# Weight halves in one tile, their columns in groups of four at a distance of sixteen, in ten of twenty units

## The chip, the cores and the metric

The kernel runs on one core of a Trainium2 chip. The metric is the device time of one execution in microseconds (us), the median of several runs.

## The reference

The reference is one attention layer with a normalisation on either side. There are 256 tokens of width 4096 and 32 heads of 128 columns, all in float32.

```python
xn   = rms_norm(x, norm_attn)                 # (256, 4096)
q, k, v, g = split(xn @ w_in_attn, 4)         # w_in_attn: 4096 x 16384
o    = stick_breaking_attention(q, k, v)      # 32 heads, strictly causal, suffix sums in log space
h    = x + (o * silu(g)) @ w_out_attn         # w_out_attn: 4096 x 4096
out  = rms_norm(h, final_norm)
```

The convolution weights of the inputs are not used at this depth. Nearly all the arithmetic lies in the two products with `w_in_attn` and `w_out_attn`.

## The kernel before

**Units and steps.** The columns of the weights are worked off in twenty units: units 0 to 15 are `w_in` (one unit holds q, k, v and gate columns of two heads), units 16 to 19 are `w_out`. A unit covers two by two blocks, and the 4096 rows are worked off in sixteen steps of 256. Units 0 and 16 ("plain") use the ordinary eight block products a step; the other eighteen ("mixed") use a scheme of seven products in most steps (Strassen's kind) and eight products in the rest. In a mixed unit of `w_in`, ten steps have seven products and six steps have eight, 118 in all. Each product is a 128x128 form of the activations (the stationary operand) times 512 weight columns (the moving operand), added up in one of seven PSUM banks `acc`.

**High and low parts.** A float32 factor is split in two parts of type fp32r, the high one and the rest, and `mm3` makes one product out of three matmuls: high by high, high by low, low by high. The weights come as `raw` tiles by DMA. In `piece` ScalarE copies `raw` to `wh` (a cast to fp32r) and VectorE subtracts, `wl = raw - wh`. A tile pair `wh`, `wl` has one or two blocks (`size` 1 or 2) of W = 512 columns, which are two halves (i = 0, 1) of CW = 256 columns from different places of the weight matrix. `split` allots them: five buffers of size 2 (tag "w"), two of size 1 (tag "s"). In steps of seven products `sums` forms three sums on VectorE in the `raw` tiles, and GpSimd issues an accumulating DMA for a fourth.

**Order.** All instructions go through a planner (`Plan`), which simulates the engines with fixed costs (`vector_ns`, `scalar_ns`, `tensor_ns`) and writes the program in the order that the simulation gives. An engine then runs its list in that order, with the waits that the data ask for. The planner's price of a matmul of n columns is

```python
def tensor_ns(n):
    return 0.4167 * n + 13.4 if n > 128 else 109.0
```

**Around it.** While unit u is multiplied, the two heads of unit u-1 are worked off between its matmuls (transposes `tr`, scores and scan `z`, output `o`), and VectorE and ScalarE empty the PSUM banks (`combine`) and do the softmax-like part. Every engine call is recorded by one helper, so all instructions bear line L121 in the profile; groups are told apart by their tiles.

Of the kernel before, what the change touches and what calls it, by code (L numbers as in the profile page):

```python
# [11 lines left out]
F32R = mybir.dt.float32r  # L12
# [7 lines left out]
P = 128  # L20
# [5 lines left out]
CW = 256  # L26
HG = CW // P
NB = D // CW
W = 2 * CW
# [27 lines left out]
ON_SCALAR = ((1, 3, 5), (1, 3))  # L57
AHEAD, SUMS_AHEAD = 4.0, 3.0
BLOCKS_LATER = 2


PLAIN = {"C11": 1, "C21": 6, "C12": 7, "C22": 3}
# [22 lines left out]
def plain_part(k, one, two):  # L85

    return k, BOTH, ((one, "A11", 0), (two, "A21", 0), (one, "A12", 1), (two, "A22", 1))
# [150 lines left out]
def kernel(  # L238
# [14 lines left out]
    wp = ctx.enter_context(tc.tile_pool(name="weights", bufs=1))  # L253
# [5 lines left out]
    ap = rooms.enter_context(tc.tile_pool(name="attention", bufs=1))  # L259
# [4 lines left out]
    def minus(out_, full, part):  # L264
        nc.vector.tensor_tensor(out=out_, in0=full, in1=part.bitcast(F32), op=ALU.subtract)
# [14 lines left out]
    for u, (kind, w, cols) in enumerate(units):  # L280
        for s in (step_at(u, k) for k in range(NS)):
            quads.append(tuple((w, c, s) for c in cols))
            if kind == "plain":
                which = [plain_part(0, PLAIN["C11"], PLAIN["C21"]), plain_part(1, PLAIN["C12"], PLAIN["C22"])]
            else:
                which = SEVEN_PARTS if s in SEVEN and not (u == LAST and s in EIGHT_LAST) else EIGHT_PARTS
# [8 lines left out]
    order = [(n, k) for n in range(n_parts - KEPT) for k in range(len(parts[n]["prods"]))]  # L295
# [4 lines left out]
    for g, (n, k) in enumerate(order):  # L300
        p = parts[n]
        b = p["u"], p["prods"][k][0]
# [8 lines left out]
    def place_at(u, s):  # L311

        return place_of[u + int(s // NS), step_at(u + int(s // NS), int(s % NS))]
# [5 lines left out]
    def dve(emit, n, key=None, **kw):  # L319
        n = n if isinstance(n, tuple) else (n,)  # L320
        cost = sum(vector_ns(m) for m in n) + 122 * (len(n) - 1)
        return nc.work("vector", cost, emit, soon() if key is None else key, **kw)

    def act(emit, n, key=None, **kw):
        n = n if isinstance(n, tuple) else (n,)
        cost = sum(scalar_ns(m) for m in n) + 100 * (len(n) - 1)
        return nc.work("scalar", cost, emit, soon() if key is None else key, **kw)
# [26 lines left out]
    raw, wh, wl = {}, {}, {}  # L354
# [42 lines left out]
    def low_done(n):  # L397
        lows_left[n] -= 1
        if not lows_left[n]:
            nc.tell(("lows", n))  # L400
            tile_done(*parts[n]["tile"])

    def sums(q):

        a, b, c, d = quad_parts[q]
        one, two = raw[q, 0], raw[q, 1]
        for k in range(2):
            tile_left[q, k] += 1

        def add(to, at_, f, g, key, op=ALU.add):  # L410
            return dve(
                lambda: nc.vector.tensor_tensor(out=to[:, :, at_, :], in0=f, in1=g, op=op), W,
                key - SUMS_AHEAD * 1e3,
            )

        yield nc.until(("lows", a), ("T3", q))
        yield add(one, 0, one[:, :, 0, :], two[:, :, 0, :], first[c], ALU.subtract)
        yield nc.until(("lows", b))
        yield add(two, 1, one[:, :, 0, :], two[:, :, 1, :], first[c])
        nc.tell(("sums", c))  # L420
        yield add(one, 1, one[:, :, 0, :], one[:, :, 1, :], first[d])
        nc.tell(("sums", d))
        for k in range(2):
            tile_done(q, k)

    def piece(n, c, there):

        p = parts[n]
        yield nc.until(*there)
        full = raw[p["tile"]][:, :, p["place"], :][:, :, c, :].rearrange("p i c n -> p c i n")  # L430
        h, l = (t[n][:, c, :].rearrange("p c (i n) -> p c i n", i=HG) for t in (wh, wl))
        size = (c.stop - c.start) * W
        key = first[n] - (AHEAD * 1e3 if p["seven"] and p["i"] < 2 else 0)
        yield act(lambda: nc.scalar.copy(h, full), size, key - 2.0 * 1e3)
        if n == 0:
            yield nc.until(("sh", c.start))
        yield dve(lambda: minus(l, full, h), size, key)
        for k in range(c.start, c.stop):
            nc.tell(("low", n, k))
        low_done(n)  # L440

    def split(size, tag, bufs):
        for n, p in enumerate(parts):
            if p["size"] != size:
                continue
            q = p["quad"]
            yield nc.take(tag)
            t = p["tile"][1]
            yield nc.until(("raw", q, t))
            wh[n] = wp.tile([P, size, W], F32R, tag=tag + "h", name=f"wh{n}", bufs=bufs)  # L450
            wl[n] = wp.tile([P, size, W], F32R, tag=tag + "l", name=f"wl{n}", bufs=bufs)
            cuts = [slice(k, k + 1) for k in range(KT)] if n == 0 else [slice(0, size)]
            lows_left[n] = len(cuts)
            if p["seven"] and p["i"] == 0:
                nc.start(sums(q))
            for c in cuts:
                nc.start(piece(n, c, [("sums", n)] if p["seven"] and p["i"] > 1 else [("raw", q, t)]))
# [51 lines left out]
    def blocks_of(i):  # L509
# [38 lines left out]
        nc.tell(("form", "s", i))  # L548
        later = place_at(0, i + BLOCKS_LATER)
        if not i:  # L550
# [211 lines left out]
    def mm3(out_, a, b, start, stop):  # L762

        (ah, al), (bh, bl) = a, b
        kw = dict(skip_group_check=True)
        nc.tensor.matmul(out_, ah, bh, start=start, stop=False, **kw)
        nc.tensor.matmul(out_, ah, bl, start=False, stop=False, **kw)
        nc.tensor.matmul(out_, al, bh, start=False, stop=stop, **kw)
# [195 lines left out]
    class Rows:  # L964


        def __init__(self, c):
            self.c = c
# [216 lines left out]
    def product(n, k):  # L1185
        p = parts[n]
        b, f, c = p["prods"][k]
        h, l = forms[p["s"]]
        mm3(
            ev[p["u"]][b],  # L1190
            (h[:, PLACES[f], :], l[:, PLACES[f], :]),
            (wh[n][:, c, :], wl[n][:, c, :]),
            starts[p["u"], b] == (n, k),
            ends[p["u"], b] == (n, k),
        )

    def products():
        for g, (n, k) in enumerate(order):
            p = parts[n]
            u, s = p["u"], p["s"]  # L1200
            b, f, c = p["prods"][k]
            if u < 1:
                what = "s"
            elif u < OUT0:
                what = "n"
            elif u == OUT0:
                what = "o"
            else:
                what = "r" if u == LAST and s in EIGHT_LAST else "p"
            if starts[u, b] == (n, k):  # L1210
                yield nc.take(f"b{b}")
                ev.setdefault(u, {})[b] = acc.tile([P, W], F32, tag=f"b{b}", name=f"acc{u}_{b}")
            yield nc.until(("low", n, c), ("form", what, s), lead=nc.LEAD)
            yield nc.work(
                "tensor", PRODUCT, lambda: product(n, k), g * PRODUCT, after=lambda n=n, k=k: done(n, k), hold=False
            )
            nc.here = g * PRODUCT

    together(split(KT, "w", PAIRS), split(1, "s", SINGLES), products(), x_stats(), x_factor(), constants())

    def in_turn(works):
# [55 lines left out]
```

## Time and profile before

| | |
|---|---|
| median of 3 runs | 1739.76 us (1739.7 to 1740.04) |
| profiled execution, first to last instruction | 1738.8 us |
| median less that span | 0.97 us |
| TensorE matmul (PE) busy | 1722.9 us, 99% |
| VectorE (DVE) busy | 1643.5 us, 95% |
| ScalarE (ACT) busy | 1204.9 us, 69% |
| HBM read | 403.98 MB, mean 237 GB/s with the writes |

The page of the profile gives the span of the profiled execution and no separate device time for it; the span lies 0.97 us under the median of the runs, so it stands for them. A row of a group shows line, engine, operation, written and read tiles, shapes and count, then busy time, mean ns of one, and idle time of the engine before it. Matmuls are pipelined: a row's mean of about 390 ns is from start to modelled end, while the next one starts some 227 ns later.

### The profile page before, as it was taken

What the parts mean: (1) busy time and instruction counts of PE and PEld (TensorE: products, weight loads), DVE (VectorE), ACT (ScalarE), POOL (GpSimd) and SP (SyncE); (2) the same over time, 40 slices, a digit from 0 to 9 for tenths busy, and PEclk for the clock granted to TensorE, in tenths of its full rate; (3) what the DMA queues carried; (4) which work ended last, traced back from release to release, by engine and by line L of the source; (5) the groups of instructions that cost most, each with busy time, mean ns of one, the idle gap of its engine ahead of it and who ended that gap; (6) DMA issues with size and microseconds to landing.
All of it is one profiled execution on the core that took longest, in us unless ns stands there. A gap on an engine that the chain in (4) does not pass through costs nothing.

```text
span 1738.8 us, 24830 instructions
## 1 busy us (share of the span) xinstructions
PE 1722.9 (99%) x7735; PEld 1412.5 (81%) x7735; DVE 1643.5 (95%) x2106; ACT 1204.9 (69%) x1640; POOL 335.5 (19%) x407
## 2 busy tenths in 40 slices
PE   9999999999999999999999999999999999999997
PEld 6888888888888888888888888888888888878885
DVE  8889999999999999999999999999999987999997
ACT  7976767676767676767676767676767675666655
POOL 0022222222222221212222222222222112221220
PEclk9999999999999999999999999999999999999999
DMA  9967788878787878787878787878787878788895
GB/s 363 297 191 227 229 231 226 230 229 236 224 234 223 240 216 238 217 251 208 255 206 255 206 256 198 257 203 259 198 256 203 269 245 265 230 268 251 233 303 191
DMA packets 249380, 413.79 MB, mean 238 GB/s; under 512 B 28128, under 2 KB 73440, under 8 KB 249248
## 3 DMA queue, kind: packets, MB, share of 16 engines
q1 hardware_dynamic: 194544, 354.24, 60.6%
q0 software_dynamic: 54416, 57.70, 20.2%
q8 instruction: 60, 0.98, 0.2%
q14 instruction: 72, 0.59, 0.1%
q10 hardware_dynamic: 288, 0.28, 0.0%
HBM read 403.98 MB, written 8.13 MB: 237 GB/s over the span
## 4 chain that ended last, share of the span: by engine, by line
PE 78%; DVE 12%; issue 6%; ACT 2%; DMA 2%; SPq 0%; DVEq 0%; ACTq 0%
PE acc L121 74%; DVE wl L121 8%; DVE raw L121 3%; PE z L121 2%; PE o L121 1%; ACT wh L121 1%; DMA raw<-in_w_in_dram 1%; PE tr L121 1%; DVE gv_sb L121 1%; DVE h L121 0%; DMA raw<-in_w_out_dram 0%; DMA grow<-in_gain_out_dram 0%; DVE qk_sb L121 0%; SPq L121 0%; ACT sq L121 0%
## 5 line engine op out<-in xcount | busy, mean ns | idle before, releaser
L121 ACT CAST wh<-raw 128x1024 fp32r<-128x1024 f32 (+1 forms) x995 | 922.0, 971 | 406.1 <-issue 180.0
L121 DVE TENSOR_TENSOR wl<-raw,wh 128x1024 fp32r<-128x1024 f32 (+1 forms) x995 | 1068.8, 1123 | 58.4 <-ACT wh L121 56.6
L121 PE MATMUL acc<-wh,sh 128*128 128x512 f32 x1898 | 755.6, 398 | 0.0
L121 PE MATMUL acc<-wl,sh 128*128 128x512 f32 x1898 | 740.0, 390 | 0.8 <-DVE wl L121 0.8
L121 PE MATMUL acc<-wh,sl 128*128 128x512 f32 x1898 | 740.5, 390 | 0.0
L121 POOL DMA_DIRECT2D raw<-in_w_in_dram x300 | 262.9, 988 | 1078.9 <-DMA raw<-in_w_in_dram 427.4
L121 PEld LDWEIGHTS acc<-wh,sl 128*128 128x128 f32 x1898 | 356.3, 188 | 75.8 <-DVE sl L121 0.4
L121 PEld LDWEIGHTS acc<-wl,sh 128*128 128x128 f32 x1898 | 357.0, 188 | 73.8 <-DVE wl L121 2.8
L121 PEld LDWEIGHTS acc<-wh,sh 128*128 128x128 f32 x1898 | 356.8, 188 | 70.7 <-ACT wh L121 0.6
L121 DVE TENSOR_TENSOR raw<-raw,raw 128x512 f32<-128x512 f32 x354 | 243.4, 687 | 6.9 <-DMA raw<-in_w_out_dram 1.2
L121 PE MATMUL acc<-wl,oh 128*128 128x512 f32 x485 | 189.7, 391 | 2.0 <-DVE wl L121 1.8
L121 PE MATMUL acc<-wh,oh 128*128 128x512 f32 x485 | 190.0, 392 | 0.0
L121 PE MATMUL acc<-wh,ol 128*128 128x512 f32 x485 | 188.9, 389 | 0.0
L121 DVE TENSOR_TENSOR raw<-raw 128x512 f32<-128x512 f32 x177 | 121.0, 684 | 0.0
L121 PEld LDWEIGHTS acc<-wl,oh 128*128 128x128 f32 x485 | 91.1, 188 | 23.8 <-DVE wl L121 5.3
L121 PEld LDWEIGHTS acc<-wh,oh 128*128 128x128 f32 x485 | 91.0, 188 | 19.2 <-DVE gv_sb L121 0.5
L121 PEld LDWEIGHTS acc<-wh,ol 128*128 128x128 f32 x485 | 91.0, 188 | 18.8
L121 POOL DMA_DIRECT2D raw<-in_w_out_dram x54 | 47.1, 968 | 185.9 <-DVE wl L121 58.9
L121 ACT ACTIVATE f<-f 128x384 f32<-128x384 f32 x96 | 50.5, 526 | 3.0
L121 ACT COPY qkT<-tr 128x512 f32<-128x512 f32 x32 | 18.6, 581 | 24.1 <-PE tr L121 24.1
L121 ACT CAST oh<-p 128x512 fp32r<-128x512 f32 (+3 forms) x46 | 20.9, 467 | 18.8 <-DVE p L121 13.2
L121 DVE SCALAR_TENSOR_TENSOR gv_sb<-acc,rin_v,gv_sb 128x512 f32<-128x512 f32 x45 | 33.4, 741 | 0.0
(91 smaller groups left out, 750.3 us busy)
## 6 DMA issues: line engine op xcount, KB each, us to landing
raw<-in_w_in_dram SPq DMA_DIRECT2D x1024, 256.0 KB, 4.5
raw<-in_w_out_dram SPq DMA_DIRECT2D x256, 256.0 KB, 4.3
raw<-in_w_in_dram POOLq DMA_DIRECT2D x300, 128.0 KB, 4.7
p<-spill POOLq DMA_DIRECT2D x28, 256.0 KB, 4.2
raw<-in_w_out_dram POOLq DMA_DIRECT2D x54, 128.0 KB, 5.1
xr<-in_x_dram SPq DMA_DIRECT2D x16, 256.0 KB, 4.8
xres<-in_x_dram SPq DMA_DIRECT2D x16, 256.0 KB, 5.6
out_dram<-h SPq DMA_DIRECT2D x16, 256.0 KB, 2.8
```

Source lines behind the costliest of these rows:

```text
L121: return self.tc.keep_in_program_order(getattr(self.engine, name)(*args, **kw))
```

## The change

The pair `wh`, `wl` becomes one tile `w` of 2 x size x 512 elements; objects of a new class `Laid` stand for its high and low part and make the access patterns. In units without an entry in `LAID` the high part lies in the first half and the low part in the second, each contiguous as before. In units 2 to 6 and 8 to 12 the 256 columns of each half lie in 64 groups of four elements (16 bytes); the groups are sixteen elements (64 bytes) apart. Four such series fill the 64 bytes. Which four they are is the layout's choice: in B and C the two halves and the two blocks c of one part (the low part lies 1024 elements later), in BB, CC and GG the two halves of the high part and of the low part (the second block lies 1024 elements later). Tiles of one block in units of B and C take BB and CC. ScalarE writes and VectorE reads and writes in that pattern, TensorE reads its moving operand in it, and the PSUM output is the same contiguous bank, seen as 2 x 64 x 4. The loads, the tiles `raw`, the activations, the planner's costs and its due times stay.

```diff
+LAYOUTS = {
+    "B": ((0, 4, 8), (1024, 4, 8)),
+    "C": ((0, 8, 4), (1024, 8, 4)),
+    "BB": ((0, 4, 1024), (8, 4, 1024)),
+    "CC": ((0, 8, 1024), (4, 8, 1024)),
+    "GG": ((0, 12, 1024), (4, 4, 1024)),
+}
+SINGLE = {"B": "BB", "C": "CC"}
+LAID = {2: "B", 8: "B", 3: "C", 9: "C", 4: "BB", 10: "BB", 5: "CC", 11: "CC", 6: "GG", 12: "GG"}
+
+class Laid:
+    def __init__(self, t, size, which, name):
+        self.t, self.size = t, size
+        if size == 1:
+            name = SINGLE.get(name, name)
+        self.base, self.block, self.row = LAYOUTS[name][which] if name else (which * size * W, 256, W)
+        self.run = (4, 16) if name else (256, 256)
+
+    def ap(self, c, row_inner=True):
+        e, step = self.run
+        c0 = c.start if isinstance(c, slice) else c
+        a = self.t[:, self.base + c0 * self.row : self.base + c0 * self.row + 1]
+        b, r = [self.block, HG], ([[self.row, c.stop - c.start]] if isinstance(c, slice) else [])
+        ap = [a.ap[0], *([b, *r] if row_inner else [*r, b]), [step, CW // e], [1, e]]
+        return bass.AP(tensor=a.tensor, offset=a.offset, ap=ap)
+
+    def like(self, t, row_inner=True):
+        e, _ = self.run
+        order = "p i c h e" if row_inner else "p c i h e"
+        return t.rearrange(f"p i c (h e) -> {order}", e=e)
...
-        full = raw[p["tile"]][:, :, p["place"], :][:, :, c, :].rearrange("p i c n -> p c i n")
-        h, l = (t[n][:, c, :].rearrange("p c (i n) -> p c i n", i=HG) for t in (wh, wl))
+        inner = LAID.get(p["u"]) not in ("B", None)
+        full = wh[n].like(raw[p["tile"]][:, :, p["place"], :][:, :, c, :], inner)
+        h, l = (t[n].ap(c, inner) for t in (wh, wl))
...
-            wh[n] = wp.tile([P, size, W], F32R, tag=tag + "h", name=f"wh{n}", bufs=bufs)
-            wl[n] = wp.tile([P, size, W], F32R, tag=tag + "l", name=f"wl{n}", bufs=bufs)
+            pair = wp.tile([P, 2 * size * W], F32R, tag=tag, name=f"w{n}", bufs=bufs)
+            wh[n], wl[n] = (Laid(pair, size, k, LAID.get(p["u"])) for k in range(2))
...
+        out_ = out_.rearrange("p (i h e) -> p i h e", i=HG, e=bh.shape[3])
...
-            (wh[n][:, c, :], wl[n][:, c, :]),
+            (wh[n].ap(c), wl[n].ap(c)),
```

## The prediction

> **What bounds the kernel now.** I read the page first: busy shares, then the chain that ended last.
>
> ```profile
> span 1738.8 us, 24830 instructions
> ...
> PE 1722.9 (99%) x7735; PEld 1412.5 (81%) x7735; DVE 1643.5 (95%) x2106; ACT 1204.9 (69%) x1640; POOL 335.5 (19%) x407
> ...
> PE 78%; DVE 12%; issue 6%; ACT 2%; DMA 2%; SPq 0%; DVEq 0%; ACTq 0%
> ```
>
> TensorE is never idle to speak of, and VectorE is only four points behind. The share of an average is not enough here, so the second view is busy time by stretch (length, then PE, PEld, DVE, ACT, POOL busy). I took unit 2 (the first changed one), unit 7 (unchanged, between the two changed groups), and the two groups themselves, units 2 to 6 and 8 to 12.
>
> ```profile
> 181.20:267.30 86.10, 86.10 (x392) 70.82 (x391) 82.98 (x102) 60.47 (x80) 18.17 (x22) 1.00 0.81 229
> 611.60:698.00 86.40, 86.40 (x392) 70.80 (x391) 83.06 (x102) 60.44 (x80) 17.60 (x22) 1.00 0.79 227
> 181.20:611.60 430.40, 430.40 (x1951) 354.01 (x1950) 414.70 (x506) 302.14 (x396) 90.38 (x106) 1.00 0.81 229
> 698.00:1128.50 430.50, 430.50 (x1952) 354.08 (x1951) 414.81 (x506) 301.45 (x394) 89.48 (x105) 1.00 0.80 229
> ```
>
> A changed unit takes 430.40 / 5 = 86.1 us, TensorE fills all of it at a granted clock of 1.00, and VectorE works 414.70 / 5 = 82.9 us of it. So two limits lie 3.1 us a unit apart, 31 us over ten units. That gap decides how much a faster TensorE can bring and how much slower VectorE may become for nothing.
>
> The third view is the chain in order of time (start, length, what), cut to one stretch, and the fourth TensorE's list around a scan.
>
> ```profile
> 499.80 27.20 PE acc L121 x120
> ```
>
> ```profile
> 283.35 0.33 PE L121 MATMUL z<-fh,neg_tri 128*128 128x384 f32 x1
> 283.52 0.34 PE L121 MATMUL z<-fl,neg_tri 128*128 128x384 f32 x1
> 283.69 0.22 PE L121 MATMUL z<-fh,neg_tri 128*128 128x128 f32 x1
> 283.75 0.28 PE L121 MATMUL z<-fl,neg_tri 128*128 128x128 f32 x1
> ```
>
> 120 matmuls of 512 columns in 27.20 us are 226.7 ns each, 0.443 ns a column. The scan's matmuls also have fp32r operands: one of 384 columns is followed 0.17 us later, again 0.44 ns a column; the one of 128 columns 0.06 us later. The planner prices a column at 0.4167 ns and calls the other 13.4 ns of a 512-column matmul fixed. At 384 columns, 0.17 us leaves 10 ns above 160, not 13: so far as two digits go, the surcharge grows with the columns. 226.7 / 0.4167 is 544, that is 17 column times for each 16 columns, and 16 float32 columns are 64 bytes: the distance at which the change sets its groups.
>
> **The change part by part.** One more row, of units 2 to 6, for what a matmul lasts from start to end:
>
> ```profile
> L121 PE MATMUL acc<-wh,sl 128*128 128x512 f32 x591 | 230.6, 390 | 0.0
> ```
>
> Order: the built program holds the same instructions in the same order on each queue (7619 on TensorE, 2108 VectorE, 1610 ScalarE, 412 GpSimd, 1353 SyncE); the loads and the planner's costs are as before. One tile in place of two adds no wait of weight, since `products` already asks for the low part before the first matmul of a product. Nineteen product matmuls now wait for an earlier matmul of TensorE itself, where fourteen transposes did; at most about 390 - 227 = 0.16 us each for the five that are new, 0.8 us, probably nothing. Units outside the ten read contiguous halves as before: nothing. What is left is what 16-byte groups at 64 bytes cost three engines. No row of this profile has such an operand, so each is bounded from both sides.
>
> *TensorE.* The rows allow two ends. If the extra column time is paid where a contiguous fetch moves on through the four 16-byte quarters of 64 bytes, a fetch that stays in one quarter for 256 columns does not pay it: 512 x 0.4167 = 213.4 ns, 13.3 ns less. If it is paid at each new 64 bytes, a matmul that meets 32 of them now meets 128: 128 x 0.4167 = 53.3 ns of surcharge, 40.0 ns more. A changed unit has 118 x 3 = 354 product matmuls: -4.7 us or +14.2 us a unit. Between the ends lies zero, if the surcharge is paid by the count of columns whatever their place.
>
> *VectorE and ScalarE.* The rows that changed units rest on, and the two lists around a wait:
>
> ```profile
> L121 DVE TENSOR_TENSOR wl<-raw,wh 128x1024 fp32r<-128x1024 f32 x210 | 245.6, 1218 | 13.0 <-ACT wh L121 12.7
> L121 ACT CAST wh<-raw 128x1024 fp32r<-128x1024 f32 x210 | 212.3, 1049 | 89.5 <-issue 41.5 <-PE acc L121 29.8 <-DVE raw L121 16.8
> L121 DVE TENSOR_TENSOR wl<-raw,wh 128x512 fp32r<-128x512 f32 x50 | 34.2, 683 | 0.0
> L121 ACT CAST wh<-raw 128x512 fp32r<-128x512 f32 x50 | 30.8, 615 | 15.3 <-issue 13.7 <-PE acc L121 1.6
> ```
>
> ```profile
> 321.72 6.97 DVE L121 TENSOR_TENSOR wl<-raw,wh 128x1024 fp32r<-128x1024 f32 x7 [0.64 <-ACT wh L121]
> ```
>
> ```profile
> 320.64 5.90 ACT L121 CAST wh<-raw 128x1024 fp32r<-128x1024 f32 x7 [3.24 <-PE acc L121]
> ```
>
> VectorE takes (1218 - 683) / 512 = 1.04 ns an element, ScalarE (1049 - 615) / 512 = 0.85 ns, both more than a TensorE column and with hardly any scatter in them. A group of four lasts 4.2 and 3.4 ns there against 1.8 ns on TensorE, so a change of place has more time to hide: I take zero. The upper end is one element time for each of the 256 groups of a 1024-element piece, 267 ns on VectorE and 217 on ScalarE. A unit has 42 such pieces and 10 of half the size, 47 in whole ones: 12.5 us and 10.2 us. Zero is covered by VectorE's 3.1 idle us as far as 3.1 / 47 = 67 ns a piece; past that point VectorE sets the unit. A gain on ScalarE would be worth little (60.5 of 86.1 us busy); one on VectorE counts only behind a faster TensorE.
>
> *The sum.* I take TensorE's lower end: 4.7 us a unit by itself. But the unit then meets VectorE: 86.1 - 82.9 leaves 3.1 us, and VectorE does not lose all its waits. It idles 13.0 / 5 = 2.6 us a unit before the subtraction, nearly all for ScalarE's cast, and the lists above show one case: the cast had waited 3.24 us for TensorE to free its buffer, VectorE 0.64 us for the cast. A faster TensorE shortens that, yet the raw tiles and VectorE's own sums still feed ScalarE. I leave 0.4 us of wait a unit: a gain of 2.75 us, 27.5 us over ten. The profiled span is 1738.8 us and the median 1739.76, so 0.97 us lies around the span and stays: 1739.8 - 27.5 = 1712.3.
>
> By the Trainium skill's page "TensorE: Matmul & The Clock Gate" (section "Wait — 56ns, not 53.3ns?"), a warm 512-column matmul follows the last by 215.7 ns, measured in bf16. The 226.7 ns above disagree by 11.0, and if 215.7 were the floor here the gain on TensorE would be 354 x 11.0 = 3.9 us a unit, an estimate that still ends at VectorE's 3.1.
>
> **Rivals.** *Each new 64 bytes costs (slower).* Place: TensorE's moving fetch in units 2 to 6 and 8 to 12. Price: 14.2 us a unit, 1739.8 + 141.6 = 1881.4 us; it decides at once, as TensorE has no slack. For it: the surcharge is exactly one in sixteen columns, and a 64-byte step is the plainest reading of that. Against it: nothing in the profile but the equal claim of the other reading. Half a column time a group would be 26.7 ns of surcharge, 13.3 more than now: 4.7 us a unit, 1787 us.
>
> *The element engines pay for the groups (slower).* Past 67 ns a piece VectorE becomes the bound; at the upper end 12.5 - 3.1 = 9.4 us a unit, 1834 us, and smaller prices give anything from 1745 up. For it: VectorE is the engine with the least slack, and each of its changed instructions has two operands in groups. Against it: its rate is a flat 1.04 ns an element in both sizes, far slower than TensorE's column.
>
> *Nothing changes.* The surcharge goes by the count of columns and the element engines don't mind: 1739.8 us, give or take 2. For it: order and waits are the same, and TensorE's surcharge is the same share at 384 and 512 columns. This is also what a rule gives: the Trainium skill's page "SBUF — State Buffer" (section "Specifications (TRN2)") has lines of 16 bytes that need two or more hits each for full bandwidth, with a penalty for crossing to a new one. A float32 group of four hits its line four times, as contiguous data do, so by that rule the change is free, 1739.8. The trace speaks half against the rule: contiguous fp32r columns do not reach the planner's column price, though each line is hit four times.
>
> **How the numbers follow.** The two ends for TensorE are about equally plain; I lean to the gain, since the layout gives the fetch the one regularity that contiguous data lack. Forecast 0.44; each new 64 bytes, or a good part of it, 0.20; the element engines 0.23; no change 0.13. A difference of 0.2%, 3.5 us, is about what a measurement of this kernel can tell from none. So faster 0.44, same 0.13, slower 0.43. The forecast's own range is 1706 (all of VectorE's slack, and a little) to 1730 (a third of the gain). With both signs likely, 8 in 10 has to reach from 1706 to the 64-byte rival: without that, more than 0.2 with the low tail would be left out. So 1706 to 1882.
>
> **What would show it.** Right: product matmuls in the changed units spaced near 213 ns (a hundred in some 21.4 us of the chain) and 227 in unit 7; those units 83 to 84 us long with VectorE busy for almost all of it, TensorE now waiting for `w` from VectorE; 1218 and 1049 ns unchanged within 20. Wrong: a spacing of about 267 ns (64-byte rival), subtractions above 1290 ns (element rival), or every row as before (no change). Should the five layouts differ among themselves, by more than 1 us between units of one group, then which quarter is read matters, and my single price for all ten fails.

## The result and the profile after

The changed kernel takes 1743.89 us (median of 10 runs, 1742.12 to 1745.69); the kernel before took 1739.73 us beside it (10 runs, 1739.21 to 1742.7). The ratio is 1.0021, 95% interval 1.0012 to 1.003: slower by 4 us where 27 us less was forecast.

From the page of the kernel after: span and instructions, busy times, and the shares of the chain that ended last.

```profile
span 1740.4 us, 24832 instructions
...
PE 1723.8 (99%) x7735; PEld 1414.5 (81%) x7735; DVE 1644.0 (94%) x2106; ACT 1205.4 (69%) x1640; POOL 335.3 (19%) x407
...
PE 73%; DVE 14%; issue 6%; DMA 3%; ACT 2%; SPq 0%; DVEq 0%; ACTq 0%
```

At this level nothing has happened: TensorE is still busy 99% and still most of the chain. The two spans, 1738.8 and 1740.4 us, differ by 1.6 us and not by 4, because the profiled execution of the kernel after took 1742.12 us, the quickest of the ten. Nearly all executions whose time and span are both on record have about 1.7 us around the span. So the execution profiled before took some 1740.5 us (an estimate), and the 0.97 us ahead of the result is a difference between two executions. The forecast added it on both sides, so it changes nothing there.

The groups of the element engines in units 2 to 6 (busy, mean ns of one, idle before):

```profile
L157 DVE TENSOR_TENSOR w<-raw,w 128x1024 fp32r<-128x1024 f32 x210 | 245.6, 1218 | 13.4 <-ACT w L157 13.4
...
L157 ACT CAST w<-raw 128x1024 fp32r<-128x1024 f32 x210 | 212.4, 1048 | 87.4 <-issue 36.1 <-PE acc L157 31.7 <-DVE raw L157 18.3
```

Before, these took 1218 and 1049 ns. Writing and reading groups of four costs VectorE and ScalarE nothing.

What did change is seen unit by unit. After its heads are done, each changed unit has one stretch of 207 product matmuls with nothing between (189 in units 7 and 13, which are contiguous). The chain in order of time (start, length, what) of the kernel after, units 2 and 4 to 12 (in unit 3 the chain runs through other engines as well):

```profile
221.84 46.82 PE acc L157 x207
394.28 46.83 PE acc L157 x207
480.29 47.72 PE acc L157 x207
566.91 47.76 PE acc L157 x207
653.45 43.21 PE acc L157 x189
739.83 46.79 PE acc L157 x207
825.81 47.51 PE acc L157 x207
912.19 46.99 PE acc L157 x207
998.42 47.79 PE acc L157 x207
1085.14 47.76 PE acc L157 x207
```

And one of them in the kernel before:

```profile
393.94 47.00 PE acc L121 x207
```

Divide each by its count: 227.0 ns a matmul before; after, 226.2 in unit 2 (layout B) and 4 (BB), 230.5 in 5 (CC), 230.7 in 6 (GG), then, from unit 8 on, 226.0 (B), 229.5 (C), 227.0 (BB), 230.9 (CC), 230.7 (GG). None is near the forecast 213 ns, none near the 267 ns of the first rival. Two layouts gain up to 1 ns a matmul and three lose 2.5 to 4.

A unit's length, counted from its first product matmul to the next unit's, says the same in microseconds:

| layout | units | before | after |
|---|---|---|---|
| B | 2, 8 | 86.1 | 85.9, 85.9 |
| C | 3, 9 | 86.1 | 86.7, 86.7 |
| BB | 4, 10 | 86.1 | 85.8, 85.8 |
| CC | 5, 11 | 86.1 | 86.9, 87.0 |
| GG | 6, 12 | 86.1 | 86.6, 86.7 |

The ten units together are 3.1 us longer; unchanged units win back 1.5 (units 7 and 13 are 0.3 us shorter each, unit 17 is 0.8). Inside a changed unit most single matmuls follow each other by 217 to 244 ns. In CC and GG (units 5 and 6) the spacings repeat every fifteen matmuls, five products, almost to the nanosecond, and in BB (unit 4) every nine; B and C show no such cycle. A cycle that repeats like this is hardly an accident of other engines and points at the places of the operands, which the experiments take up.

### The profile page after: what moved, and what is told of

It reads as the page before. It is cut to its first block, busy times and chain, and to the rows that moved or that the text cites. A ratio compares the mean times of both kernels' runs of the same rounds, so it can differ in the third digit from the quotient of the medians.

```text
span 1740.4 us, 24832 instructions
## 1 busy us (share of the span) xinstructions
PE 1723.8 (99%) x7735; PEld 1414.5 (81%) x7735; DVE 1644.0 (94%) x2106; ACT 1205.4 (69%) x1640; POOL 335.3 (19%) x407
## 4 chain that ended last, share of the span: by engine, by line
PE 73%; DVE 14%; issue 6%; DMA 3%; ACT 2%; SPq 0%; DVEq 0%; ACTq 0%
PE acc L157 69%; DVE w L157 9%; DVE raw L157 3%; DMA raw<-in_w_in_dram 2%; ACT w L157 2%; PE z L157 2%; PE o L157 1%; DVE gv_sb L157 1%; DMA raw<-in_w_out_dram 1%; PE tr L157 1%; DMA xres<-in_x_dram 0%; DVE qk_sb L157 0%; DVE h L157 0%; SPq L157 0%; DMA grow<-in_gain_out_dram 0%
## 5 line engine op out<-in xcount | busy, mean ns | idle before, releaser
L157 ACT CAST w<-raw 128x1024 fp32r<-128x1024 f32 (+1 forms) x995 | 922.0, 971 | 402.4 <-issue 165.6
L157 PE MATMUL acc<-w,sh 128*128 128x512 f32 x3796 | 1190.0, 394 | 1.7 <-DVE w L157 1.0
L157 DVE TENSOR_TENSOR w<-raw,w 128x1024 fp32r<-128x1024 f32 (+1 forms) x995 | 1068.6, 1122 | 59.6 <-ACT w L157 58.2
L157 PEld LDWEIGHTS acc<-w,sh 128*128 128x128 f32 x3796 | 704.3, 188 | 147.5 <-DVE w L157 3.6
L157 PE MATMUL acc<-w,sl 128*128 128x512 f32 x1898 | 738.2, 389 | 0.0
L157 PEld LDWEIGHTS acc<-w,sl 128*128 128x128 f32 x1898 | 356.4, 188 | 76.2 <-DVE sl L157 0.6
L157 PE MATMUL acc<-w,oh 128*128 128x512 f32 x970 | 301.8, 391 | 1.5 <-DVE w L157 1.3
L157 PEld LDWEIGHTS acc<-w,oh 128*128 128x128 f32 x970 | 181.4, 188 | 42.0 <-DVE w L157 4.2
L157 PE MATMUL acc<-w,ol 128*128 128x512 f32 x485 | 188.9, 389 | 0.0
L157 PEld LDWEIGHTS acc<-w,ol 128*128 128x128 f32 x485 | 91.0, 188 | 18.8
```

The lines of the kernel that those rows point to most:

```text
L157: return self.tc.keep_in_program_order(getattr(self.engine, name)(*args, **kw))
```

## The experiments

Two questions were open after the result. What sets the surcharge over the planner's column price, if neither the count of columns nor the quarters explain it? And had it gone, would the unit have become shorter? Diffs are against the kernel after unless another is named; each ratio is to the kernel before. "Spacing" is the mean distance between the starts of product matmuls that follow one another, from the trace, without the distances above 280 ns, at which TensorE waited or had other work; where a line of the chain is shown, it is its length divided by its count.

**1. The parts of the change: shared tile, and one layout everywhere.**

```diff
-LAID = {2: "B", 8: "B", 3: "C", 9: "C", 4: "BB", 10: "BB", 5: "CC", 11: "CC", 6: "GG", 12: "GG"}
+LAID = {}                              # one_tile
+LAID = {u: "B" for u in range(20)}     # all_B; all_BB and all_CC alike
```

> Changed kernel with no unit laid out: high and low part share a tile, both contiguous. If the layouts alone move the time: 1739.7 us, within 2 us of the kernel before, product matmuls spaced 227 ns in all units. If the shared tile and the few waits that moved with it carry the loss: 1742 to 1744 us with the 227 ns spacing unchanged.

> Layout B in all twenty units (BB for tiles of one block). The units with B and BB were 0.2 to 0.3 us shorter in the changed kernel's trace (85.8 to 85.9 us against 86.1), those with C, CC and GG 0.5 to 0.9 longer. If a unit's layout sets its length whatever its neighbours have: about 20 x -0.25 = -5 us, 1735 us. If the loss comes with any layout by groups, from run to run: 1742 us or more.

> Layout BB in all twenty units. In the changed kernel's trace its two units took 85.8 us against 86.1 before, the best of the five layouts; with B in all units the mixed ones came to 86.0. If the unit's own layout sets its length: 18 x -0.3 = -5 us or a little more, 1734 to 1735 us. If the small differences of B and BB are no more than the scatter of the phases: as all B, 1737 us.

> Layout CC in all twenty units. Its two units were 0.85 us longer than contiguous ones in the changed kernel's trace. If the unit's own layout sets its length: 18 x 0.85 = 15 us and a little for the plain units, 1755 us. If lengths depend on what the neighbouring units have: nearer to the changed kernel, 1740 to 1746 us.

| run | median us | ratio |
|---|---|---|
| one_tile | 1740.47 | 0.9999 [0.999, 1.0009] |
| all_B | 1736.95 | 0.9978 [0.9968, 0.9987] |
| all_BB | 1737.51 | 0.9986 [0.9977, 0.9995] |
| all_CC | 1757.22 | 1.0091 [1.0074, 1.0108] |

The shared tile alone changes nothing: its spacing is 227.0 ns, as before. So the layouts carry the result, and they have opposite signs. CC everywhere loses 17 us. This is close to the 1755 us expected, but in part by luck: the mixed units of `w_in` last 86.6 us in most cases, 0.5 us more than before and not 0.85, and 7.5 of the 17.4 us that the span grows by are lost in the four units of `w_out`. B everywhere beats both kernels, yet by 3.8 us only. The chain of all_CC, then that of all_B, each with one stretch:

```profile
570.00 47.75 PE acc L157 x207
```

```profile
392.70 46.76 PE acc L157 x207
```

230.7 and 225.9 ns a matmul. BB everywhere ends where B does, not at the 1734 to 1735 us that its 85.8 us a unit in the changed kernel promised: its units now last 86.0 us. What all_B does with its gain is told at experiment 6.

**2. The place of the stationary operand.** The theory then was that the weight load, which runs beside the matmul before it, collides with the moving fetch when both want the same part of a memory row. These kernels leave the weights as they are and take the stationary operand from other places, so they compute other products. The first two take 128 columns of the weight tile itself at a step of sixteen elements; the others take one column of the activations, repeated.

```diff
-            (h[:, PLACES[f], :], l[:, PLACES[f], :]),
+            ... if p["size"] == 1 else (wh[n].t[:, 0::16],) * 2,                  # bb_w0; 8::16 in bb_w2
+            tuple(t[:, PLACES[f], 0:1].broadcast_to([P, P]) for t in (h, l)),     # bb_b0, plain_b0; 8:9 in bb_b2
```

LAID is "BB" everywhere in the `bb_` kernels and empty in plain_b0.

> Layout BB in all units, and the stationary operand of every product on a two-block tile is replaced by 128 weight values, each sixteenth element from element 0 of the pair's tile, so that all weight loads read the first 16-byte quarter of each 64 bytes (the output is therefore another one; the instructions are the same in number). Moving high parts lie in quarters 0 and 1, low parts in 2 and 3. Theory of collision (a matmul's moving fetch loses time where the weight load that runs beside it reads the same quarter): high-by-low matmuls, whose moving columns avoid quarter 0, come down to 213 to 218 ns; the two with a moving high part rise above 230. Theory of the moving fetch alone: the stationary operand plays no part, each of the three keeps the 220 to 234 ns of the changed kernel's BB units. Count of columns: 227 everywhere.

> As the run before it, but the stationary operand is read from the third quarter (element 8, each sixteenth). Collision: the picture turns round, the two matmuls with a moving high part come down to 213 to 218 ns and the one with the moving low part rises above 230. Moving fetch alone: no difference from the run before it.

> Contiguous weights in one tile, as in the run without layouts, but the stationary operand of every weight product is one column of the activations 128 times over (step 0), so that a weight load reads one 16-byte place in place of 512 bytes in a row; the output is therefore another one. Collision of moving fetch and weight load: the surcharge of 13 ns falls, the spacing goes from 227 to 214 to 218 ns and the span to 1700 us or so, where VectorE takes over. Surcharge of the moving fetch alone, or by the count of columns: 227 ns as before, 1739 us.

> Layout BB in all units, stationary operand one column 128 times over, from the first 16-byte quarter (element 0 of the form). Collision with a load that reads its place again for each column: high-by-low matmuls (moving quarters 2 and 3) 214 to 218 ns, the other two 225 or more. Collision with a load that reads its place once: all three 214 to 218. Moving fetch alone: the 220 to 234 ns of the changed kernel's BB units.

> As the run before it, with the column from the third quarter (element 8). Collision with repeated reads: the picture turns round, high-by-low 225 or more and the other two 214 to 218. Collision with a single read: all three 214 to 218. Moving fetch alone: no difference from the run before it.

Each was timed once: bb_w0 1751.42 us, bb_w2 1793.68, plain_b0 1757.41, bb_b0 1774.12, bb_b2 1744.73; all_BB, with the same moving operands, took 1737.51. The first pair spoilt its own test. The weight loads of bb_w0 in unit 4, a stepped and a contiguous group (mean ns is the second number after the bar):

```profile
L157 PEld LDWEIGHTS acc<-w 128*128 128x128 f32 x302 | 70.2, 301 | 0.4
L157 PEld LDWEIGHTS acc<-w,sh 128*128 128x128 f32 x18 | 3.3, 188 | 0.3
```

A stepped load lasts 301 ns, more than the distance from one matmul to the next, so each load's record reaches into the next one's; whether the load itself became part of the bound is not shown. The expected pattern over the three matmuls of a product did not show (means of 230, 228.5 and 229 ns in bb_w0; 236, 232.5 and 238 in bb_w2). Still, the two differ by 42 us, and only by the place from which the load reads and the values that stand there.

The columns that are repeated load in 189 ns, so there the test is clean. The chain of bb_b0:

```profile
577.44 48.74 PE acc L157 x207
```

235.5 ns a matmul. By the three matmuls of a product (high by high, high by low, low by high; the stationary factor first) the means in this stretch are 246, 219 and 243 ns, against 223, 228 and 228 in all_BB. The two that move the high part, whose groups stand in the quarters where the column stands, are slow; the one that moves the low part, two quarters away, is fast. That was expected of the collision. Its mirror image did not appear in bb_b2: there the means are 231, 225 and 231 ns, in a cycle over five products. And plain_b0, where a fall to 214 to 218 ns was expected, rose. Its chain:

```profile
573.01 47.96 PE acc L157 x207
```

231.7 ns. The cleanest pair is bb_b0 and bb_b2: the same loads in number and length, 32 bytes apart, and 29 us between them. So the stationary operand alone moves the spacing of matmuls whose moving operand is the same, which is shown, and by its place, if the values that it holds are of no account (both runs have a granted clock of 0.998; experiment 4 moves places without changing a value). The simple rule for it (same quarter slow, other quarter fast) fails in two of three runs.

The Trainium skill's page "TensorE: Matmul & The Clock Gate" (section "Step-by-step: what each phase is for") says that TensorE has two independent read ports, so that loading the next weights takes no read bandwidth from the running matmul. By that rule bb_b0 would have run as all_BB; it was 36.6 us slower, with loads of the same length, so these runs do not agree with it.

**3. The size and the distance of the groups.** Each unit got a layout of its own: `two(e)` puts the two halves in groups of e elements in turn, `four(e)` the halves of both parts, `parts_of(e)` the two parts; `shifted(s)` stays contiguous and begins s elements later.

```diff
+def two(e):
+    return lambda size: ((0, size * W), e, 2 * CW, e, 2 * e, True)
+LAID = {2: four(4), 3: two(4), 4: two(8), 5: two(16), 6: two(32), 7: four(8), 8: four(16), 9: four(2), 10: two(2), 11: parts_of(4), ...
```

> Fourteen layouts in one kernel, one for each of units 2 to 15 (all other units contiguous). Unit 2 is BB (groups of 4, distance 16). Units 3 to 6 interleave the two halves of a part alone, groups of 4, 8, 16, 32 at twice their length; units 7, 8, 9 interleave halves and parts as BB does, groups of 8, 16 and 2 at four times their length; unit 10 halves alone, groups of 2; units 11 and 12 high with low part, groups of 4 and 16 at twice their length; units 13, 14, 15 contiguous, begun 4, 8 and 12 elements further on than the tile. Contiguous units took 86.1 us (86.3 in 14 and 15), BB 85.8. Collision of moving fetch and weight load by place and phase: lengths differ from arm to arm by 0.5 us or more within groups of 4 and 8, a layout whose groups are whole multiples of 64 bytes goes back to 86.1, and a mere shift by a quarter moves the spacing off 227. Moving fetch alone: the shifted units keep 227 ns and 86.1 to 86.3 us. A group of 2 meets each 16-byte line twice in place of four times: if a line costs, units 9 and 10 are the longest by far, over 95 us.

The chain of this run, the long stretches of the two units with groups of two elements, unit 9 (`four(2)`) and unit 10 (`two(2)`):

```profile
875.82 95.47 PE acc L163 x207
1042.90 92.44 PE acc L163 x207
```

461 and 447 ns a matmul. Groups of two double the time: 461 / 256 = 1.8 ns for each group of 8 bytes, and contiguous data cost 226.7 / 128 = 1.77 ns per 16 bytes. All groups of four and more lie between 85.9 us a unit (`four(4)`) and 90.0 (`two(16)`, `four(16)`). This fits a price for each 16-byte line that TensorE fetches, about 4.25 column times, and groups of four or more never add a line. It is not the only reading: a price for each group, in the moving operand or in the output, which is written in the same groups, would double the time as well, and no run starts a group off a 16-byte boundary to tell them apart. VectorE does not mind groups of two (1225 ns), and ScalarE takes 6% longer (1116 ns). The whole run took 1929.92 us. Unit 1 of this run, contiguous as ever, took 87.0 us instead of 85.7. Its tiles had grown by 64 bytes, so that each buffer began at another place; that was the first sign of what follows.

The Trainium skill's page "SBUF — State Buffer" (section "Specifications (TRN2)") asks for two or more hits on a 16-byte line for full bandwidth. For TensorE's moving operand in fp32r this run does not agree that two are enough: two hits a line give half the rate (461 and 447 ns), four give all of it.

**4. The relative place of the two operands.** In place1 and place2 every tile begins at the place that it has in the kernel after modulo 512 bytes, and each unit moves the weights in its tiles of two blocks by a number of elements; tiles of one block stay. Six raw buffers make the room, so only the spacing is compared.

```diff
-RAW_BUFS = 7
+RAW_BUFS = 6
+LAID = {2: shifted(4), 3: shifted(8), 4: shifted(12), 5: shifted(16), 6: shifted(32), 7: shifted(64), 8: shifted(96), ...
-            pair = wp.tile([P, 2 * size * W], F32R, tag=tag, name=f"w{n}", bufs=bufs)
+            pair = wp.tile([P, 2 * size * W + 128 * (size - 1)], F32R, tag=tag, name=f"w{n}", bufs=bufs)
```

> The place of the weights within 512 bytes, unit by unit; pair tiles get 512 bytes more (six raw buffers in place of seven make the room, so waits for data may differ: the spacing of matmuls in a row is what is read). In all kernels so far with 227 ns in contiguous units the pair tiles and the tiles of the activations began at the same byte of 512 (416), and in the kernel of fourteen layouts, where they did not, contiguous units had 225 to 237 ns. Units 2 to 8: contiguous, both parts begun 4, 8, 12, 16, 32, 64, 96 elements later; 9 and 10: the low part alone 8 and 64 elements later; 11 to 15: BB begun 0, 8, 32, 64, 96 elements later; units 0, 1 and 16 to 19 contiguous without a shift. If the relative place in 512 bytes decides: unit 1 at 227, the shifted contiguous units at 229 to 235 on the mean, with places that differ from each other by some ns. If only the place in 64 bytes decides: shifts of 16, 32, 64, 96 elements leave 227. If the place is nothing and the drift from buffer to buffer mattered: 227 in all contiguous units.

> As the run before it: BB begun 4, 12, 16, 24, 48, 112 elements later in units 2 to 7; B begun 0, 4, 8, 16, 32, 64, 96 elements later in units 8 to 14; contiguous begun 120 elements later in unit 15. If the relative place in 512 bytes decides, BB and B have one best place, at 218 to 224 ns on the mean, and worst ones at 230 to 235; if only the place in 64 bytes does, 16, 48, 112 and 32, 64, 96 are like 0; if neither, all are at 226 ns as in the kernels with BB or B everywhere.

Spacing in ns against the shift in elements of four bytes:

| shift | 0 | 4 | 8 | 16 | 32 | 64 | 96 |
|---|---|---|---|---|---|---|---|
| contiguous | 227.5 | 231.7 | 233.0 | 231.5 | 232.6 | 227.5 | 232.5 |
| BB | 226.5 | 230.5 | 228.5 | 228.2 | 229.4 | 226.6 | 229.6 |
| B | 226.3 | 232.0 | 228.4 | 228.0 | 229.7 | 226.0 | 229.5 |

Shift 64, which is 256 bytes, gives back the value of shift 0, to 0.3 ns in all three forms, and every other shift is worse. A best place at 218 to 224 ns, which place2 expected if the place decided, was not found. Shift 0 is the place that the kernel before has by chance of its allocation, and it is the good one.

The cleanest proof changes no instruction. To the kernel before, one empty tile is added ahead of the activations:

```diff
     sp = ctx.enter_context(tc.tile_pool(name="stationary", bufs=1))
...
+    sp.tile([P, 32], F32, name="pad")     # pad128; [P, 64] in pad256
```

> The kernel before (contiguous weights, separate tiles) with one empty tile of 128 bytes between the weights and the activations; no instruction differs. Place within 256 bytes decides: the spacing goes from 227 to 231 to 233 ns, units from 86.1 to 87.3 to 87.6 us, the kernel to about 1763 us (1740 + 18 x 1.3). Something else did it in the shifted units: 1740 us.

> As the run before it with a tile of 256 bytes. Place within 256 bytes decides: 227 ns and 1740 us as before. A longer period or any displacement decides: 1750 us or more.

pad128 takes 1767.62 us, ratio 1.0155 [1.0138, 1.0172]; pad256 takes 1740.22, ratio 0.9998 [0.9989, 1.0008]. The chains, pad128 first, then pad256:

```profile
312.81 48.30 PE acc L121 x207
400.37 48.30 PE acc L121 x207
```

```profile
307.45 47.00 PE acc L121 x207
393.55 47.00 PE acc L121 x207
```

An empty 128 bytes makes each matmul 233.3 ns and each unit 87.6 us long, an empty 256 bytes leaves 227.1 and 86.1. So the surcharge of contiguous weights goes by the place of the weights and the activations, modulo 256 bytes. That it is the place of one against the other is the plainest reading, since moving the weights by 128 bytes (232.6 ns) and moving the activations by 128 bytes give nearly the same; a run that moves both together was not made.

**5. Looking for a place without surcharge.** place3 spreads one block pair over eight series 128 bytes apart, and tries further shifts of the low part; all_B_sl16 and all_B_sl48 are all_B with the low parts of the activations moved by 64 and 192 bytes.

```diff
+def eight(l, block, row, inner):
+    return lambda size: ((0, l), block, row, 4, 32, inner) if size == 2 else four(4)(size)
```

```diff
+    sh_pool = ctx.enter_context(tc.tile_pool(name="highs", bufs=1))
+    sp.tile([P, 16], F32, name="pad")     # all_B_sl16; 48 in all_B_sl48
-        h = sp.tile([P, n, P], F32R, tag=f"xh{i}", name=f"{what}h{i}")
+        h = sh_pool.tile([P, n, P], F32R, tag=f"xh{i}", name=f"{what}h{i}")
```

> All at the aligned place but for what is named (padded pair tiles and six raw buffers again). Units 2 to 5: eight series in groups of 4 at a distance of 32, halves, blocks and parts in four orders; units 6, 7, 8: B with the low part 16, 32, 48 elements further on; units 9, 10, 11: the two halves interleaved, groups of 4, 8, 16; units 12, 13: high with low, groups of 4 and 8; unit 14 BB's scheme with groups of 8; unit 15 contiguous, low part 16 further on. Collision by place: contiguous order keeps the 227 ns because both streams walk the same 256 bytes in step; a fetch with fewer places (a distance of 32) meets the load more seldom but longer, 222 to 230 ns on the mean; shifted low parts are between 226 and 232; interleaved orders whose groups are 8 or 16 lie nearer to 227 than in the kernel of fourteen layouts, where they had 233 to 240. If the place of the groups were nothing and only alignment counted: all of units 2 to 5 and 9 to 14 at 226 to 227.5.

> Layout B in all units, the tiles of the activations' low parts in a pool of their own, 16 elements further on within 256 bytes than the high parts. The moving low part then lies 48 elements further on (of 64) against the stationary low part, as in the unit of the run before that had 225.2 ns on the mean against 225.8 to 226.1 for B. Place of the two against each other decides: 0.2 to 0.3 us a unit less than all B, 1732 to 1733 us. Only the weights' own order decides: all B's 1737 us.

> The same with 48 elements in place of 16: the moving low part lies 16 elements further on against the stationary low part, as in the unit that had 225.75 ns. Place of the two against each other decides: 0 to 0.1 us a unit less than all B, 1735 to 1737 us. Only the weights' own order decides: 1737 us.

place3 found nothing near 213 ns. Groups 128 bytes apart are the worst of all forms of four (249.6 to 251.4 ns in four orders, where 222 to 230 was expected). The start is not all that counts: the two halves in turn in groups of 4, 8 and 16 elements, begun at the good place, have 231.6, 232.4 and 239.9 ns. B with its low part 16 or 48 elements on has 226.1 and 225.4 (225.75 and 225.2 in the expectations, which count slightly otherwise), the latter the best spacing seen in a whole unit up to then. Moved activations do about what moved weights did in all_B_sl16 (225.2 to 226.0 in the mixed units) and not quite in all_B_sl48 (226.3 to 226.7). all_B_sl16 takes 1736.69 us, ratio 0.9981 [0.9972, 0.999], all_B_sl48 1738.23, 0.9988 [0.9979, 0.9997]: neither is told apart from all_B, and the 1732 to 1733 us expected of all_B_sl16 did not come.

**6. Would a faster TensorE have helped?** In all_B the matmuls follow each other more closely than before (226.4 against 227.3 ns over 201 spacings of the long stretch, 232.3 against 234.7 over 143 others), together 0.5 us a unit, but units last 86.0 us, 0.1 less than before: 0.4 come back at the 46 spacings of the heads' matmuls, where TensorE waits. To see what holds them, short_lh takes the kernel before and runs the third matmul of each product on 256 of its 512 columns, so that half of low by high is left out:

```diff
-        nc.tensor.matmul(out_, al, bh, start=False, stop=stop, **kw)
+        nc.tensor.matmul(out_[:, 0:CW], al, bh[:, 0:CW], start=False, stop=stop, **kw)
```

> The kernel before with the third matmul of each product (low by high) on 256 of its 512 columns, so that TensorE has 118 x 113 ns = 13.4 us less to do in a unit (half of that term is left out of the output). Nothing else differs; the plan and the order are the same. It shows what the units would take if TensorE lost any surcharge. The prediction's slack (VectorE busy 82.9 of 86.1 us and 0.4 us of waits that stay): mixed units of w_in at 83.3 us, the kernel below 1695 us. If VectorE's idle 3.1 us are part of a chain that does not depend on TensorE (casts that wait for VectorE's sums, instructions that only wait or signal): 86.0 us a unit as with B everywhere, some 1730 us.

It took 1729.86 us in its one run. Busy time by stretch, 181 to 611 us (length, then PE, PEld, DVE, ACT, POOL), in the kernel before, in all_B and in short_lh:

```profile
181.00:611.00 430.00, 430.00 (x1950) 353.67 (x1949) 414.31 (x506) 301.74 (x395) 89.98 (x106) 1.00 0.81 229
```

```profile
181.00:611.00 430.00, 429.18 (x1952) 353.12 (x1951) 414.66 (x506) 302.43 (x395) 90.28 (x105) 1.00 0.81 230
```

```profile
181.00:611.00 430.00, 393.29 (x1952) 321.10 (x1951) 414.65 (x506) 302.31 (x396) 90.37 (x105) 0.98 0.81 230
```

In short_lh TensorE has 37 us less to do in these 430 us, and the same number of matmuls is done in them (1952 against 1950). The units are no shorter: units 2 to 6, and 7 to 11 likewise, last 86.0 us on average (84.6 to 87.4 each). The 9.9 us that the whole kernel gains come from the plain units 0 and 16, which are 9.0 and 8.5 us shorter; units behind them give a good part back. The granted clock in this stretch is 0.98 instead of 1.00, which is small beside TensorE's 37 us. VectorE's work is the same to 0.4 us in all three. The waits in the same stretch (total, times, longest) of the kernel before and of short_lh:

```profile
DVE wl L121 <- ACT wh L121: 12.7, 25, 0.6
```

```profile
PEld acc L121 <- DVE wl L121: 21.5, 28, 1.3
...
PE acc L121 <- DVE wl L121: 12.8, 22, 1.0
DVE wl L121 <- ACT wh L121: 12.6, 25, 0.6
```

VectorE's wait for the cast is the same 25 waits and 12.6 us with TensorE relieved; TensorE now waits for VectorE. Apart from 0.8 us, again for ScalarE, the profile names no other wait of VectorE in this stretch, neither for TensorE nor for a DMA. VectorE's list and ScalarE's list around two such waits in short_lh show what they are:

```profile
397.12 1.42 DVE L121 TENSOR_TENSOR raw<-raw,raw 128x512 f32<-128x512 f32 x2
398.45 0.68 DVE L121 TENSOR_TENSOR raw<-raw 128x512 f32<-128x512 f32 x1
399.77 6.97 DVE L121 TENSOR_TENSOR wl<-raw,wh 128x1024 fp32r<-128x1024 f32 x7 [0.64 <-ACT wh L121]
406.66 1.41 DVE L121 TENSOR_TENSOR raw<-raw,raw 128x512 f32<-128x512 f32 x2
407.99 0.68 DVE L121 TENSOR_TENSOR raw<-raw 128x512 f32<-128x512 f32 x1
409.31 3.50 DVE L121 TENSOR_TENSOR wl<-raw,wh 128x1024 fp32r<-128x1024 f32 x3 [0.64 <-ACT wh L121]
```

```profile
398.69 5.89 ACT L121 CAST wh<-raw 128x1024 fp32r<-128x1024 f32 x7 [3.24 <-PE acc L121]
408.23 3.47 ACT L121 CAST wh<-raw 128x1024 fp32r<-128x1024 f32 x4 [3.65 <-issue]
```

VectorE's pair of sums ends at 397.12 + 1.42 = 398.54 us, and the cast begins at 398.69; the next pair ends at 408.07, and the cast begins at 408.23. The distance is 0.15 to 0.16 us both times, though the profile names TensorE as the releaser of the one and nothing ("issue") as that of the other. In the kernel before the same pair ends at 406.56 and the cast begins at 406.71, and this is so in all_B too (405.31, 405.47). So the sum releases the cast. The cast takes 1.05 us, VectorE has one more sum of 0.68 to do meanwhile, and the rest, 0.64 us, it waits before it can subtract. VectorE waits for itself by way of ScalarE, and TensorE is not in the loop. Three of the five waits of a unit are of this kind, 1.9 us together, with the same 0.15 to 0.16 us between sum and cast each time. The other two (0.44 and 0.18 us) come behind ScalarE's work for the heads and are also as long as before. So these 2.5 of the 3.1 us in which VectorE idles in a unit are no slack, and in this order of instructions a unit without a TensorE bound lasts 86.0 us on average, 0.1 less than in the kernel before. all_BB, all_B, all_B_sl16 and all_B_sl48 all stand at this 86.0, whether their long stretches run at 226.2 or 226.7 ns. It is a mean and not a limit for each unit: single units in B and BB took 85.8 to 85.9 us in the changed kernel. That they drew on time that VectorE had gained in slower units is likely, but not shown.

## Why the prediction was wrong

**The step that failed first is TensorE's lower end.** The prediction read 226.7 ns as 512 columns and a toll for walking through four quarters of 64 bytes, and took -13.3 ns for groups that stay in one quarter. Measured: -1 ns in B and BB, +2.5 to +4 in C, CC and GG. The row that it rested on was right (544 column times), the cause was not. For contiguous weights the toll goes by where weights and activations lie modulo 256 bytes, as the two pads and the shifted weights show. It is also not the count of columns, which the prediction held as the value between its ends: the same 512 columns take 225 to 251 ns in groups of four at various places. The prediction looked at one operand only and never at the address of the other.

**The step that failed second is VectorE's slack.** The prediction took 86.1 - 82.9 = 3.1 us a unit as room to be gained, kept back 0.4 us of wait, and argued from a cast that stood as waiting 3.24 us for TensorE that a faster TensorE shortens VectorE's wait. The releaser in that row was taken at its word: short_lh has the same 3.24 us with the same name on it and TensorE relieved. The wait did not shorten at all, and the floor is 86.0 us. Ten units at the floor would have gained about 1 us, not 27.5. So the forecast would have failed even with the toll gone; and all_B shows it from the other side: its matmuls save 0.5 us a unit and the unit 0.1. Of all_B's 4.7 us of span only 1.4 are won in units 2 to 13; 0.5 come from unit 0, 0.8 from unit 1 and 1.9 from the four units of `w_out`.

**Right** were the steps priced at nothing: the shared tile and the moved waits (one_tile, 0.9999), and VectorE and ScalarE in groups (1218 and 1048 ns). "Nothing changes", 1739.8 give or take 2, was the nearest rival, 4 us off, but by cancellation, not for the reason given: two layouts gain 0.2 to 0.3 us a unit and three lose 0.5 to 0.9. The first rival's 64-byte toll (267 ns) and the element engines' rival are not seen in any of the five layouts. The prediction's last condition, that layouts which differ by more than 1 us would overthrow its single price, was met (85.8 to 86.9 us in units 2 to 6) and pointed at the right question.

**What stays open.** In B and BB the two halves stand in neighbouring quarters, in C and CC two quarters apart, in GG three apart in the high part and in neighbouring ones in the low part; the first two gain, the others lose. No rule from places to nanoseconds was found that also gives bb_b2 and plain_b0. That the weight load beside the matmul is the other party to the collision is supported by the 29 us between bb_b0 and bb_b2 and the 42 us between bb_w0 and bb_w2; how the two collide was not shown. Some 215 to 218 ns is the least seen for single matmuls; why no layout keeps it up is open.

## What to carry to other kernels

Before pricing an access pattern, ask where both operands lie: here an empty tile of 128 bytes cost 27 us, more than any rearrangement gained, so test the relative place of the two operands (a pad of a few sizes) before touching layouts. Idle time on the second-busiest engine is slack only if its releaser would come earlier; follow each wait back, and if the chain returns to the same engine, the loop is a floor until the order of its instructions is changed. To learn what a faster engine would bring, make its work smaller by a crude cut first: one run of that kind would have shown 86.0 us before any layout was thought of.

## What was not expected of the hardware

- Matmuls in fp32r of 512 columns cost 227 to 233 ns contiguous, by the place of their operands, with a period of 256 bytes in the shifts tried.
- Groups of two elements in the moving operand cost 447 to 461 ns a matmul, groups of four 225 to 251 ns by place.
- A weight load whose columns stand 64 bytes apart lasts 301 ns, a contiguous one 188 ns.
- VectorE and ScalarE work in groups of four, and nearly in groups of two, at their contiguous speed.
